# A hybrid decoder step: the first two columns of the recurrent input run over half the tokens first

## The chip, the cores and the metric

One core of one Trainium2 chip runs the whole program in one launch. The metric is the device time of that launch in microseconds (us), the median of the runs. The engines are named as in the profile: PE is TensorE, DVE is VectorE, ACT is ScalarE, POOL is GpSimd, and SP is the engine that issues nearly all transfers.

## The reference, cut to what matters

The model is one inference step of a two-layer decoder over 512 prompt tokens and 8 sample tokens, 520 in all, with 1024 channels. Layer 0 begins with an RG-LRU block:

```python
h = rms_norm(x, g_mix[0])
proj = h @ w_in                    # 1024 -> 2 * 1280
y = gelu(proj[..., :D_RNN])
xr = proj[..., D_RNN:]             # the recurrent input
xc = causal_dwconv(concat([conv_hist, xr]), conv_w, conv_b)   # width 4
r, i = sigmoid(xc blocks @ w_a + b_a), sigmoid(xc blocks @ w_x + b_x)
```

After it come the recurrence, its output product, a gated feed-forward block and an embedding, then a second layer with sparse attention. The change touches only the beginning: reading x, the first norm and the first three of the ten blocks of 128 channels of xr.

## The kernel before, in words

Activations stand with channels on the partitions: x is a tile of 128 partitions by 8 blocks by 520 tokens. Float32 products are made of three fast ones: each operand is split into a high part (ACT rounds it) and a low part (DVE subtracts the high part), and high times high, high times low and low times high are summed in PSUM. `split` (line 150) does this for weights, `xg_part` (line 500) for x times the norm's gain g_mix. The norm's other factor, one over the root mean square of a token, is multiplied in later, when a product leaves PSUM (`evac_scaled`, line 449).

One "column" is 128 output channels over all 520 tokens. `emit_k` (line 351) issues for each of the 8 blocks of input channels three products of two halves of 260 tokens: 48 matmuls a column, into one two-bank PSUM tile `MM`. There are three `MM` tiles and two one-bank tiles `TR`. `dense` (line 363) runs columns one after another. Its argument `at` hooks work in behind a block k of the first column. A column may start only when the `MM` tile of the column three before it has been read out.

The weights come through `Stream` (line 225). A chunk is loaded into one of three `RAW` tiles by SP, then split unit by unit (a unit is one column's weights) into `W` tiles, of which there are eight. The four row blocks of x (128 tokens by 1024 channels each) also stand in `W` tiles, and the 8 sample rows stand in a `RAW` tile whose other half is the scratch of the square sums.

Lines 510 to 550 are the fill. They stand in a block in which the order is written out by hand on each engine; instructions from outside the block may be put between by the planner. SP issues the identity matrix, x rows 0, the first 16 vectors, x rows 1, the sample rows, x rows 2, the first column's weights (`ws.load_to(0)`), x rows 3, the second column's weights (`add_second`), two tables and chunk 1. PE transposes a row block (`x_block`, line 187) by eight 128x128 transposes through the two `TR` tiles, and DVE or ACT copies each bank into x. Then `xg_part` splits blocks 0 to 3 of the first 256 tokens on ACT and DVE, blocks 4 to 7 on ACT and POOL, and all eight of the other 264 tokens on ACT and DVE. `x_square` (line 182) sums squares on ACT; four of the five stand behind all this, then `nm.root` makes the norm's factor on DVE. Three `dense` calls run columns 0, 1 and 2. Inside column 2, behind k = 1, `nm.bcast` (line 423) transposes the factor so that it stands beside the tokens, five PE transposes and two ACT copies.

Behind the block, `post_xr` (line 592) takes the three products out of PSUM, multiplied by that factor, and makes the convolution; columns 3 to 9 follow in the same way, then the gates. Small work that stands outside the block is `rg_scales` (line 205, some twenty DVE instructions on 128x10), the loading of the page table (line 572, eight small transfers on SP) and two DVE instructions on it (lines 575 and 576).

Of the kernel before, what the change touches and what calls it, by code (L numbers as in the profile page):

```python
# [20 lines left out]
NS = 8  # L21
# [93 lines left out]
def kernel(ctx: ExitStack, tc: tile.TileContext, I, O):  # L115
# [28 lines left out]
    def k3(ap, a):  # L144
        return ap.rearrange("p (a b) -> p a b", a=a)
# [40 lines left out]

    def x_block(tb):
        rows = 128 if tb < 4 else NS
        for q in range(0, 8, 4):
            ps = TR()  # L190
            for a in range(4):
                pe.transpose(ps[:, a * rows:(a + 1) * rows],
                             raws_x[tb][:rows, (q + a) * 128:(q + a + 1) * 128], ident[:rows, :rows])
            eng = act.copy if q and tb != 3 else dve.tensor_copy
            eng(x[:, q:q + 4, tb * 128:tb * 128 + rows], k3(ps[:, :4 * rows], 4))

    voff = {n: sum(r for _, r in VECS[:q]) for q, (n, _) in enumerate(VECS)}
    def V(name, i=0):
        c = voff[name] + i
        return vec[:, c:c + 1]  # L200
# [259 lines left out]

    # ---- weights, in the order in which the tensor engine takes them
    rgo = [("g", m) for m in range(10)] + [("y", m) for m in range(10)]
# [31 lines left out]

    # ---- layer 0, first norm, first columns of the recurrent input
    xg = [(T(F32R), T(F32R)) for _ in range(8)]
    xps, nm = [], Norm()
    ssq = sml[:, 48:53]

    def xg_part(j, c0, c1, eng):  # L500
        h, l = (t[:, c0:c1] for t in xg[j])
        act.activation(h, x[:, j, c0:c1], AF.Copy, scale=V("g_mix", j))
        if eng is dve:
            dve.scalar_tensor_tensor(l, x[:, j, c0:c1], V("g_mix", j), f32(h), op0=OP.mult, op1=OP.subtract)
        else:
            tm = T()[:, c0:c1]
            eng.tensor_mul(tm, x[:, j, c0:c1], V("g_mix", j).to_broadcast([128, c1 - c0]))
            eng.tensor_sub(l, tm, f32(h))

    with tc.manual_schedule():  # L510
        sp.dma_start(ident, I["consts"][:, 0:128])
        x_rows(0)
        sp.dma_start(vec[:, 0:16], I["vecs"][:, 0:16])
        x_rows(1)
        x_rows(4)
        x_rows(2)
        ws.load_to(0)
        x_rows(3)
        add_second()
        sp.dma_start(vec[:, 16:530], I["vecs"][:, 16:530])  # L520
        sp.dma_start(cst[:, 128:CCOS], I["consts"][:, 128:CCOS])
        ws.load_to(1)
        dve.memset(onesf, 1.0)
        dve.memset(ssq, 1.0)
        act.activation(sml[:, 40:41], onesf[:, 0:1], AF.Square)
        x_square(0, ssq)
        x_block(0)
        x_block(1)
        x_block(4)
        for j in range(4):  # L530
            xg_part(j, 0, 256, dve)
        x_block(2)
        ws.ahead(1)
        for j in range(4, 8):
            xg_part(j, 0, 256, pool)
        x_block(3)
        for j in range(8):
            xg_part(j, 256, NT, dve)
        ws.ahead(2)
        for tb in (1, 4, 2, 3):  # L540
            x_square(tb, ssq)
        y = nm.root(ssq)
        top, ws.stop = ws.stop, 2
        rst = []
        dense(1, 8, xg, lambda n, ps: xps.append(ps))
        dense(2, 8, xg, lambda n, ps: xps.append(ps), n0=1)
        ws.stop = 3
        dense(3, 8, xg, lambda n, ps: xps.append(ps), n0=2, at={1: lambda: rst.append(nm.bcast(y, 0))})
        rstd = rst[0]
        ws.stop = top  # L550

    # ---- states of the RG-LRU
    rg_t, rg_p, rg_o = T(), T(), T()
# [12 lines left out]

    # ---- page table, gathers
    pti = P.tile([128, 8], I32, name="pti")
# [15 lines left out]

    # ---- the recurrent input, its convolution
    st_c = k3(rg_o[:, 0:110], 11)
# [5 lines left out]
    def post_xr(m, ps):  # L592
        xr, xc = T(), T()
        pool.memset(xr[:, 0:3], 0.0)
        evac_scaled(xr[:, 3:3 + NT], ps, rstd)
        act.activation(xc[:, :NT], xr[:, 3:3 + NT], AF.Identity, scale=V("rg_conv_w", 30 + m), bias=V("rg_conv_b", m))
        pool.tensor_copy(st_c[:, :, m], xr[:, NP:NP + 11])
        xq.append((m, xr, xc))
        if m:
            conv_split(*conv_xr())  # L600
# [100 lines left out]

    # what the other engines do while the tensor engine is at each column of the gate branch
    SLOTS = ["e0 e1 r0 e2 r1 e3 r2", "e4 r3 e5 r4 e6 r5", "e7 r6 e8 r7 e9 r8 r9",
# [206 lines left out]

    # ---- compression weights
    w1h = [[T(F32R) for _ in range(4)] for _ in range(2)]
# [84 lines left out]

    # ---- token-major keys and values of the prompt and of the sample
    vst = [[T(F32R), T(F32R)] for _ in range(2)]
# [40 lines left out]

    # ---- compressed keys and values: the cache of the sample, then the prompt
    skh, skl = T(F32R), T(F32R)
# [309 lines left out]

    # ---- sample attention: scores
    kst, k0 = {}, {}
# [324 lines left out]

    # ---- first columns of the attention's output product, with the last heads  # L1680
    wo, wps = [], []
# [232 lines left out]
    yw, ys, fin = {}, [], {}  # L1914
    hcols = [(0, 256), (256, NT)]

# [136 lines left out]
```

## Time and profile before

| | |
|---|---|
| time, median of 3 runs | 1691.95 us (1690.61 to 1693.42) |
| the profiled execution: its time from first to last instruction (span) | 1690.5 us; the page gives no other time of it |
| lowest run less that span | 0.11 us |
| PE busy | 1628.7 us, 96% of the span |
| first matmul of a product starts | 15.50 us |
| last matmul of column 2 has started by | 35.70 us |

The span is read as the time between the program's first and last instruction; what a run has around it can be at most the difference to the lowest run, if both executions were alike. Times inside the program are us from the start of the span. A timeline row gives start, duration and count of like instructions that follow each other; what stands in brackets is how long the engine was idle before them and what ended that.

### The profile page before, as it was taken

The numbers are of one execution on the slowest core, as the hardware profiler recorded it, in microseconds if no ns is written. First come the engines' busy times: TensorE is split into PE (matmuls) and PEld (weight loads), VectorE is DVE, ScalarE is ACT, GpSimd is POOL, SyncE is SP. The second block draws the span as 40 slices with busy tenths as digits, with TensorE's granted clock in tenths as the row PEclk, the third lists the DMA queues.
The fourth block names the chain that finished last, engine by engine and source line by source line (L and its number), as shares of the span: only waits on it lengthen the run. The fifth ranks groups of instructions, "written<-read, shape, count | busy, mean of one in ns | idle before, by whom it ended". The sixth has DMA issues, their size and how long they took to land.

```text
span 1690.5 us, 32157 instructions
## 1 busy us (share of the span) xinstructions
PE 1628.7 (96%) x13089; PEld 1593.8 (94%) x13089; DVE 1081.3 (64%) x1794; ACT 795.7 (47%) x1455; POOL 410.9 (24%) x652
## 2 busy tenths in 40 slices
PE   7988999999999999999999999989999999999997
PEld 7988999999999999989999788869999999999997
DVE  6879647645654663665777878785576366466445
ACT  5674434423432444435743777783343144134434
POOL 2266411100100112321023466562111011001113
PEclk9999999999999999999998999999999999999998
DMA  6242343233233232334232213203332332332311
GB/s 197 86 148 89 107 128 93 83 101 93 82 101 95 81 113 81 96 120 142 80 123 100 94 41 116 76 26 85 101 90 85 100 91 85 101 90 85 112 32 51
DMA packets 197746, 160.81 MB, mean 95 GB/s; under 512 B 8160, under 2 KB 189872, under 8 KB 194760
## 3 DMA queue, kind: packets, MB, share of 16 engines
q1 hardware_dynamic: 194576, 136.74, 26.7%
q0 software_dynamic: 3024, 22.02, 3.6%
q8 instruction: 103, 1.69, 0.4%
q14 instruction: 43, 0.35, 0.1%
HBM read 154.41 MB, written 8.98 MB: 97 GB/s over the span
## 4 chain that ended last, share of the span: by engine, by line
PE 80%; DVE 8%; ACT 5%; issue 3%; POOL 2%; DMA 0%; SPq 0%; DVEq 0%; POOLq 0%; ACTq 0%
PE mm L355 62%; PE sc L355 2%; PE o L1648 2%; DVE w L155 1%; PE tr L1616 1%; ACT t L1590 1%; PE sc L1566 1%; ACT w L152 1%; PE tr L1516 1%; PE mm L1103 1%; PE mm L1104 1%; PE mm L1105 1%; DVE x L868 1%; PE tr L1087 1%; PE o L355 1%
## 5 line engine op out<-in xcount | busy, mean ns | idle before, releaser
L355 PE MATMUL mm<-t,w 128*128 128x260 f32 x9984 | 1214.9, 284 | 18.7 <-DVE t L455 9.8
L355 PEld LDWEIGHTS mm<-t,w 128*128 128x128 f32 x9984 | 1208.0, 189 | 21.5 <-issue 7.9
L152 ACT ACTIVATE w<-raw 128x1024 fp32r<-128x1024 f32 (+2 forms) x230 | 232.6, 1014 | 338.4 <-PE mm L355 287.0
L155 DVE TENSOR_TENSOR w<-raw,w 128x1024 fp32r<-128x1024 f32 (+2 forms) x230 | 282.5, 1232 | 65.3 <-ACT w L152 58.8
L455 DVE TENSOR_TENSOR t<-mm,t 128x520 f32<-128x520 f32 x138 | 95.6, 696 | 139.6 <-PE mm L355 136.0
L812 POOL COPY t<-t 128x10 f32<-128x10 f32 x96 | 24.0, 250 | 616.6 <-DVE t L455 616.6
L785 DVE TENSOR_TENSOR x<-x,mm 128x520 f32<-128x520 f32 x61 | 42.4, 696 | 170.2 <-PE mm L355 170.1
L815 DVE SCALAR_TENSOR_TENSOR t<-t,vec 128x512 f32<-128x512 f32 x192 | 143.1, 748 | 3.9 <-POOL t L812 0.7
L152 ACT ACTIVATE t<-t 128x520 fp32r<-128x520 f32 (+5 forms) x100 | 58.9, 593 | 182.8 <-DVE t L825 125.9
L155 DVE TENSOR_TENSOR t<-t 128x520 fp32r<-128x520 f32 (+5 forms) x100 | 69.1, 696 | 53.0 <-ACT t L152 52.7
L396 POOL TENSOR_TENSOR t<-t 128x520 f32<-128x520 f32 x35 | 57.5, 1644 | 171.2 <-ACT t L392 161.2
L155 DVE TENSOR_TENSOR w<-tr,w 128x512 fp32r<-128x512 f32 (+1 forms) x120 | 71.1, 612 | 27.1 <-ACT w L152 26.6
L813 ACT ACTIVATE t<-t,vec 128x520 f32<-128x520 f32 x96 | 78.8, 823 | 7.0 <-DVE t L455 7.0
L824 ACT ACTIVATE t<-t 128x520 f32<-128x520 f32 x48 | 30.6, 638 | 89.6 <-DVE t L815 89.5
L152 ACT ACTIVATE w<-tr 128x512 fp32r<-128x512 f32 (+1 forms) x120 | 60.6, 545 | 23.0 <-PE tr L1087 12.6
L1608 POOL TENSOR_TENSOR t<-t,sm 128x384 f32<-128x384 f32 (+1 forms) x64 | 59.8, 955 | 36.4 <-DVE sm L1600 18.5
L1590 ACT ACTIVATE t<-sc,sm 128x384 f32<-128x384 f32 (+3 forms) x120 | 63.1, 535 | 8.6 <-DVE sm L1577 4.6
L817 POOL TENSOR_TENSOR t<-t 128x8 f32<-128x8 f32 x96 | 46.7, 487 | 59.4 <-ACT t L813 59.2
L1616 PE MATMUL tr<-cst,t 128*128 128x128 f32 x320 | 56.2, 286 | 2.0 <-DVE sm L1600 2.0
L355 PE MATMUL sc<-t,w 128*128 128x260 f32 (+1 forms) x336 | 53.5, 283 | 0.7 <-ACT t L1108 0.7
L1566 PE MATMUL sc<-t 128*128 128x384 f32 (+1 forms) x128 | 41.1, 422 | 10.2 <-ACT t L1590 9.7
L152 ACT ACTIVATE t<-tr 128x128 fp32r<-128x128 f32 (+4 forms) x85 | 29.9, 374 | 40.9 <-PE tr L1316 18.8
(401 smaller groups left out, 1896.8 us busy)
## 6 DMA issues: line engine op xcount, KB each, us to landing
raw<-in_ffn_w_up SPq DMA_DIRECT2D x96, 512.0 KB
raw<-in_ffn_w_down SPq DMA_DIRECT2D x24, 1024.0 KB
raw<-in_ple_w_gate SPq DMA_DIRECT2D x8, 1024.0 KB
raw<-in_rg_w_in SPq DMA_DIRECT2D x12, 512.0 KB
raw<-in_rg_w_out SPq DMA_DIRECT2D x8, 640.0 KB
raw<-in_rg_w_in SPq DMA_DIRECT2D x4, 1024.0 KB
raw<-in_attn_w_qg SPq DMA_DIRECT2D x4, 1024.0 KB
t<-in_cache_win_kv SPq DMA_DIRECT2D x16, 256.0 KB
```

What stands on the lines that cost most here:

```text
L152: act.activation(hi, src, AF.Copy)
L155: (lo_eng or dve).tensor_sub(lo, src, f32(hi))
L355: pe.matmul(half(ps, hf)[:m, 0:HN], w[:, ki, :m], xx[:, hf * HN:(hf + 1) * HN], start=first and q == 0, stop=last and q == 2)
L396: (dve if self.n == 7 else pool).tensor_add(self.acc[:, :NT], self.acc[:, :NT], sq[:, :NT])
L455: dve.tensor_mul(halves(dst), ps[:m, :, 0:HN], halves(r[:m, :NT]))
L813: act.activation(t[:, :NT], up[:, 2:2 + NT], AF.Identity, scale=V("ffn_conv_w", 144 * i + 96 + j), bias=V("ffn_conv_b", 48 * i + j))
L815: dve.scalar_tensor_tensor(t[:, :NP], up[:, 2 - d:2 - d + NP], V("ffn_conv_w", 144 * i + (2 - d) * 48 + j), t[:, :NP], op0=OP.mult, op1=OP ...
L817: pool.tensor_add(t[:, NP:NT], t[:, NP:NT], pv[:, j, :])
L1566: pe.matmul(pss[br][:, 0:n], l, kst[br, g][q][:, 0:n], start=q == 0, stop=False)
L1590: act.activation(p[br][:, 0:n], sv[br], AF.Exp, bias=s[:, 0, br:br + 1], accum_out=s[:, 1, br:br + 1])
L1608: pool.tensor_mul(v, v, s[:, 3, br:br + 1].to_broadcast([128, n]))
L1616: pe.transpose(ps[:, j * 128:(j + 1) * 128], p[br][:, j * 128:(j + 1) * 128], ident)
```

## The change

The first two columns are computed first for the tokens 0 to 255, as soon as x rows 0 and 1 are there, and for the other 264 tokens afterwards.

- SP: the weights of the first two columns are issued behind x rows 1, ahead of the sample rows and x rows 2 and 3.
- x rows 0 and 1 are transposed into four PSUM banks (the two `TR` tiles and one `MM` tile), two channel blocks to a bank. ACT (`xg_hi`) and DVE (`xg_lo`) split x times gain straight from these banks. The copies into x come behind the splits, three on DVE and the last on ACT. POOL has no part in the fill any more.
- The weight splits of the first two columns are done in quarters of four blocks (`first_split`), the second column's into `T` tiles, and their order stands by hand between the other work. `first_mm` runs 24 matmuls of 256 (then 264) tokens into one bank of the column's `MM` tile.
- The sample rows and x rows 2 and 3 are transposed behind that, each before the next piece of products. The other 264 tokens are split when x rows 3 are copied.
- The square sums stand one behind each row block, and that of x rows 3 behind the weight split of column 2. `nm.bcast` moves from behind k = 1 to behind k = 5 of column 2.
- In `post_xr` the columns 0 and 1 are taken out of PSUM in two instructions, and without the raised priority of `evac_scaled`.

```diff
--- before.py
+++ after.py
@@ -184,15 +184,19 @@
         act.activation(raws_x[4][:rows, 1024:2048], raws_x[tb][:rows, 0:1024], AF.Square,
                        accum_out=out[:rows, tb:tb + 1])
 
-    def x_block(tb):
+    def x_t(ps, tb, j):
         rows = 128 if tb < 4 else NS
-        for q in range(0, 8, 4):
+        pe.transpose(ps, raws_x[tb][:rows, j * 128:(j + 1) * 128], ident[:rows, :rows])
+
+    def x_block(tb, engs):
+
+        rows = 128 if tb < 4 else NS
+        for q in range(0, 8, 4 if tb < 4 else 8):
+            n = 4 if tb < 4 else 8
             ps = TR()
-            for a in range(4):
-                pe.transpose(ps[:, a * rows:(a + 1) * rows],
-                             raws_x[tb][:rows, (q + a) * 128:(q + a + 1) * 128], ident[:rows, :rows])
-            eng = act.copy if q and tb != 3 else dve.tensor_copy
-            eng(x[:, q:q + 4, tb * 128:tb * 128 + rows], k3(ps[:, :4 * rows], 4))
+            for a in range(n):
+                x_t(ps[:, a * rows:(a + 1) * rows], tb, q + a)
+            engs[q // 4](x[:, q:q + n, tb * 128:tb * 128 + rows], k3(ps[:, :n * rows], n))
 
     voff = {n: sum(r for _, r in VECS[:q]) for q, (n, _) in enumerate(VECS)}
     def V(name, i=0):
@@ -492,64 +496,105 @@
     add_ffn(1)
     add_dense(I["ple_w_gate"][1], 8, 0, 8)
 
+
     xg = [(T(F32R), T(F32R)) for _ in range(8)]
     xps, nm = [], Norm()
     ssq = sml[:, 48:53]
 
-    def xg_part(j, c0, c1, eng):
-        h, l = (t[:, c0:c1] for t in xg[j])
-        act.activation(h, x[:, j, c0:c1], AF.Copy, scale=V("g_mix", j))
-        if eng is dve:
-            dve.scalar_tensor_tensor(l, x[:, j, c0:c1], V("g_mix", j), f32(h), op0=OP.mult, op1=OP.subtract)
-        else:
-            tm = T()[:, c0:c1]
-            eng.tensor_mul(tm, x[:, j, c0:c1], V("g_mix", j).to_broadcast([128, c1 - c0]))
-            eng.tensor_sub(l, tm, f32(h))
+    hcols = [(0, 256), (256, NT)]
+
+    def xg_hi(j, hf, src):
+        c0, c1 = hcols[hf]
+        act.activation(xg[j][0][:, c0:c1], src, AF.Copy, scale=V("g_mix", j))
+
+    def xg_lo(j, hf, src):
+        c0, c1 = hcols[hf]
+        dve.scalar_tensor_tensor(xg[j][1][:, c0:c1], src, V("g_mix", j), f32(xg[j][0][:, c0:c1]),
+                                 op0=OP.mult, op1=OP.subtract)
+
+    def first_mm(hl, ps, hf, k0, k1):
+        c0, c1 = hcols[hf]
+        for k in range(k0, k1):
+            h, l = (t[:, k % 4, :] for t in hl[k // 4])
+            for q, (w, xx) in enumerate(((h, 0), (h, 1), (l, 0))):
+                pe.matmul(ps[:, hf, 0:c1 - c0], w, xg[k][xx][:, c0:c1], start=k == 0 and q == 0,
+                          stop=k == 7 and q == 2)
 
     with tc.manual_schedule():
         sp.dma_start(ident, I["consts"][:, 0:128])
         x_rows(0)
         sp.dma_start(vec[:, 0:16], I["vecs"][:, 0:16])
         x_rows(1)
+        ws.load_to(0)
+        add_second()
         x_rows(4)
         x_rows(2)
-        ws.load_to(0)
         x_rows(3)
-        add_second()
         sp.dma_start(vec[:, 16:530], I["vecs"][:, 16:530])
         sp.dma_start(cst[:, 128:CCOS], I["consts"][:, 128:CCOS])
         ws.load_to(1)
         dve.memset(onesf, 1.0)
         dve.memset(ssq, 1.0)
         act.activation(sml[:, 40:41], onesf[:, 0:1], AF.Square)
+        raw = k3(ws.raws[0], 8)
+        t0, t1 = W(), W()
+        fw = [[tuple(k3(t, 8)[:, 4 * q:4 * q + 4, :] for t in (t0, t1)) for q in range(2)],
+              [tuple(k3(T(F32R)[:, 0:512], 4) for _ in range(2)) for q in range(2)]]
+
+        def first_split(n, q):
+            split(raw[:, 4 * q:4 * q + 4, n * 128:(n + 1) * 128], *fw[n][q])
+
+
+        banks = [TR(), TR()]
+        mm = MM()
+        banks += [mm[:, 0, :], mm[:, 1, :]]
         x_square(0, ssq)
-        x_block(0)
-        x_block(1)
-        x_block(4)
-        for j in range(4):
-            xg_part(j, 0, 256, dve)
-        x_block(2)
-        ws.ahead(1)
-        for j in range(4, 8):
-            xg_part(j, 0, 256, pool)
-        x_block(3)
+        for tb in range(2):
+            for j in range(8):
+                x_t(banks[j // 2][:, (j % 2) * 256 + tb * 128:(j % 2) * 256 + tb * 128 + 128], tb, j)
+        x_square(1, ssq)
+        xps.append(MM())
+        for r, bank in enumerate(banks):
+            src = k3(bank, 2)
+            for a in range(2):
+                xg_hi(2 * r + a, 0, src[:, a, :])
+            for a in range(2):
+                xg_lo(2 * r + a, 0, src[:, a, :])
+            if r < 2:
+                first_split(0, r)
+            if r < 3:
+                dve.tensor_copy(x[:, 2 * r:2 * r + 2, 0:256], src)
+            if r:
+                first_mm(fw[0], xps[0], 0, 2 * r - 2, 2 * r)
+        first_mm(fw[0], xps[0], 0, 6, 8)
+        act.copy(x[:, 6:8, 0:256], src)
+        del banks, bank, src, mm
+        x_block(4, (dve.tensor_copy,))
+        xps.append(MM())
+        for q in range(2):
+            first_split(1, q)
+        x_square(4, ssq)
+        x_block(2, (dve.tensor_copy, act.copy))
+        first_mm(fw[1], xps[1], 0, 0, 8)
+        x_square(2, ssq)
+        x_block(3, (dve.tensor_copy, act.copy))
         for j in range(8):
-            xg_part(j, 256, NT, dve)
-        ws.ahead(2)
-        for tb in (1, 4, 2, 3):
-            x_square(tb, ssq)
+            xg_hi(j, 1, x[:, j, 256:NT])
+            xg_lo(j, 1, x[:, j, 256:NT])
+        first_mm(fw[0], xps[0], 1, 0, 8)
+        first_mm(fw[1], xps[1], 1, 0, 8)
+        del raw, fw, t0, t1, ws.raws[0]
+        ws.nsplit = ws.used = 2
+        top, ws.stop = ws.stop, 3
+        ws.ahead()
+        x_square(3, ssq)
         y = nm.root(ssq)
-        top, ws.stop = ws.stop, 2
         rst = []
-        dense(1, 8, xg, lambda n, ps: xps.append(ps))
-        dense(2, 8, xg, lambda n, ps: xps.append(ps), n0=1)
-        ws.stop = 3
-        dense(3, 8, xg, lambda n, ps: xps.append(ps), n0=2, at={1: lambda: rst.append(nm.bcast(y, 0))})
+        dense(3, 8, xg, lambda n, ps: xps.append(ps), n0=2, at={5: lambda: rst.append(nm.bcast(y, 0))})
         rstd = rst[0]
         ws.stop = top
 
-    # ---- states of the RG-LRU
+
     rg_t, rg_p, rg_o = T(), T(), T()
     sp.dma_start(rg_t[:, 0:320], I["rg_state"])
     hst = rg_t[:, 0:240].rearrange("p (k m b) -> p k m b", k=3, m=10)
@@ -592,7 +637,11 @@
     def post_xr(m, ps):
         xr, xc = T(), T()
         pool.memset(xr[:, 0:3], 0.0)
-        evac_scaled(xr[:, 3:3 + NT], ps, rstd)
+        if m < 2:
+            for hf, (c0, c1) in enumerate(hcols):
+                dve.tensor_mul(xr[:, 3 + c0:3 + c1], ps[:, hf, 0:c1 - c0], rstd[:, c0:c1])
+        else:
+            evac_scaled(xr[:, 3:3 + NT], ps, rstd)
         act.activation(xc[:, :NT], xr[:, 3:3 + NT], AF.Identity, scale=V("rg_conv_w", 30 + m), bias=V("rg_conv_b", m))
         pool.tensor_copy(st_c[:, :, m], xr[:, NP:NP + 11])
         xq.append((m, xr, xc))
...
-    hcols = [(0, 256), (256, NT)]
```

## Rows read from the trace of the kernel before

**Rows 1.** The page: the span, the busy time of four engines (share of the span, instructions), and the shares of the chain of work that ended last.

```profile
span 1690.5 us, 32157 instructions
PE 1628.7 (96%) x13089; PEld 1593.8 (94%) x13089; DVE 1081.3 (64%) x1794; ACT 795.7 (47%) x1455; POOL 410.9 (24%) x652
...
PE 80%; DVE 8%; ACT 5%; issue 3%; POOL 2%; DMA 0%; SPq 0%; DVEq 0%; POOLq 0%; ACTq 0%
```

**Rows 2.** The timeline of PE from 4 to 45 us: start, us, instruction, count.

```profile
4.65 1.94 PE L192 MATMUL tr<-cst,w 128*128 128x128 f32 x8 [4.65 <-DMA w<-in_x_prompt]
7.14 1.57 PE L192 MATMUL tr<-cst,w 128*128 128x128 f32 x8 [0.55 <-DMA w<-in_x_prompt]
9.01 0.78 PE L192 MATMUL tr<-cst,raw 8*128 8x8 f32 x8 [0.30 <-DVE x L195]
9.72 1.09 PE L192 MATMUL tr<-cst,w 128*128 128x128 f32 x8
12.27 1.94 PE L192 MATMUL tr<-cst,w 128*128 128x128 f32 x8 [1.45 <-DMA w<-in_x_prompt]
15.50 13.69 PE L355 MATMUL mm<-t,w 128*128 128x260 f32 x100 [1.30 <-ACT t L502]
29.85 1.24 PE L355 MATMUL mm<-t,w 128*128 128x260 f32 x8 [0.66 <-DVE w L155]
30.93 0.60 PE L427 MATMUL tr<-cst,nrm 128*128 128x128 f32 x4
31.36 0.27 PE L430 MATMUL tr<-cst,nrm 128*128 128x128 f32 x1
```

**Rows 3.** The same view for the rest of column 2 alone (31.38 to 35.70 us): its last 36 matmuls.

```profile
31.39 4.58 PE L355 MATMUL mm<-t,w 128*128 128x260 f32 x36
```

**Rows 4.** Stretches of the fill: stretch, its us, busy us of PE, PEld, DVE, ACT and POOL (instructions), the granted share of PE's full clock (0.50 is 1.2 GHz, 1.00 is 2.4 GHz), the busy share of the DMA engines, GB/s.

```profile
4.60:6.60 2.00, 1.94 (x8) 1.57 (x8) 0.69 (x1) 1.15 (x2) 0.00 (x0) 1.00 0.90 304
8.20:11.60 3.40, 2.31 (x21) 1.76 (x19) 2.03 (x5) 2.35 (x7) 0.61 (x1) 1.00 1.08 354
11.60:15.00 3.40, 1.94 (x8) 1.57 (x8) 3.06 (x6) 3.10 (x8) 1.41 (x2) 0.50 1.10 352
15.00:18.40 3.40, 2.90 (x13) 2.87 (x14) 3.40 (x5) 3.40 (x9) 3.24 (x5) 0.50 0.59 195
18.50:28.40 9.90, 9.90 (x84) 9.90 (x83) 9.05 (x44) 7.89 (x13) 1.32 (x2) 1.00 0.49 163
```

**Rows 5.** The timeline of ACT, the rows of the operations that the change moves or repeats.

```profile
4.60 1.06 ACT L184 ACTIVATE raw<-w 128x1024 f32<-128x1024 f32 x1 [2.38 <-DMA w<-in_x_prompt]
5.57 0.19 ACT L184 ACTIVATION_READ_ACCUMULATOR raw<-w 128x1 f32 x1
...
9.91 1.71 ACT L502 ACTIVATE t<-x,vec 128x256 fp32r<-128x256 f32 x4
11.52 0.57 ACT L195 COPY x<-tr 128x512 f32<-128x512 f32 x1
11.98 1.06 ACT L152 ACTIVATE w<-raw 128x1024 fp32r<-128x1024 f32 x1
...
23.71 1.06 ACT L184 ACTIVATE raw<-w 128x1024 f32<-128x1024 f32 x1
...
31.56 0.59 ACT L428 COPY t<-tr 128x512 f32<-128x512 f32 x1 [1.81 <-PE tr L427]
32.05 0.17 ACT L431 COPY t<-tr 128x8 f32<-128x8 f32 x1
```

**Rows 6.** The timeline of DVE, the rows of the operations that the change moves or repeats.

```profile
9.46 0.19 DVE L195 COPY x<-tr 128x32 f32<-128x32 f32 x1 [0.50 <-PE tr L192]
10.46 1.68 DVE L504 SCALAR_TENSOR_TENSOR t<-x,vec,t 128x256 fp32r<-128x256 f32 x4 [0.80 <-ACT t L502]
...
13.08 1.23 DVE L155 TENSOR_TENSOR w<-raw,w 128x1024 fp32r<-128x1024 f32 x1 [0.34 <-ACT w L152]
14.22 1.28 DVE L195 COPY x<-tr 128x512 f32<-128x512 f32 x2
15.48 3.80 DVE L504 SCALAR_TENSOR_TENSOR t<-x,vec,t 128x264 fp32r<-128x264 f32 x5
...
19.84 1.29 DVE L504 SCALAR_TENSOR_TENSOR t<-x,vec,t 128x264 fp32r<-128x264 f32 x3
```

**Rows 7.** The timeline of DVE from the end of the norm's factor to the page table, and at the end of the ten columns.

```profile
28.49 0.16 DVE L419 SCALAR_TENSOR_TENSOR nrm<-nrm 128x5 f32<-128x5 f32 x1
28.57 4.63 DVE L155 TENSOR_TENSOR w<-raw,w 128x1024 fp32r<-128x1024 f32 x4
33.12 1.29 DVE L455 TENSOR_TENSOR t<-mm,t 128x520 f32<-128x520 f32 x2
...
40.29 0.17 DVE L575 CAST ptf<-pti 128x8 f32<-128x8 int32 x1 [3.31 <-DMA pti<-in_page_table]
...
42.50 0.69 DVE L455 TENSOR_TENSOR t<-mm,t 128x520 f32<-128x520 f32 x1
...
76.61 0.70 DVE L455 TENSOR_TENSOR t<-mm,t 128x520 f32<-128x520 f32 x1 [0.17 <-PE mm L355]
```

**Rows 8.** Two groups of `rg_scales` by line: count, then busy us and mean ns of one, then idle us before them.

```profile
L218 DVE TENSOR_SCALAR sml<-sml 128x10 f32<-128x10 f32 x7 | 1.2, 172 | 0.2
L217 DVE TENSOR_TENSOR sml<-sml 128x10 f32<-128x10 f32 x7 | 1.2, 170 | 0.2
```

**Rows 9.** The timeline of SP's queue: the loads of chunks 2 and 3 (one row), and the page table behind them.

```profile
22.58 2.67 SPq L282 DMA_DIRECT2D raw<-in_rg_w_in  x2
25.30 1.05 SPq L573 DMA_DIRECT2D pti<-in_page_table  x2
```

**Rows 10.** PE behind the ten columns: its timeline with the stalls of the gates, and the stretch 80 to 120 us with the columns of rows 4.

```profile
69.77 17.03 PE L355 MATMUL mm<-t,w 128*128 128x260 f32 x139
88.77 9.91 PE L355 MATMUL mm<-t,w 128*128 128x260 f32 x68 [1.97 <-ACT t L648]
100.53 6.02 PE L355 MATMUL mm<-t,w 128*128 128x260 f32 x48 [1.84 <-DVE t L610]
```

```profile
80.00:100.00 20.00, 16.71 (x124) 16.18 (x122) 14.23 (x11) 13.42 (x23) 17.20 (x12) 0.91 0.39 120
100.00:120.00 20.00, 17.11 (x140) 16.91 (x141) 14.60 (x12) 15.09 (x21) 12.89 (x9) 1.00 0.56 177
```

## The prediction

> **What bounds the kernel now.** I read the page first. PE is busy for 96% of the span and carries 80% of the chain that ended last [rows 1], so a microsecond counts only where it lets PE go on earlier. The change works in the first 36 us, so I read PE's timeline there next [rows 2]. Up to 15.50 us PE has only transposes, and it waits between them: for x rows, for the copies out of PSUM, and last for the split. From 15.50 us it is dense. 96 products of columns 0 and 1 and the first four of column 2 run to 29.19 us, 0.66 us are lost to a weight split on DVE, and column 2 ends with 36 matmuls from 31.39 us [rows 2, 3]. At 0.12 us each these are issued by 35.8 us, and column 3 follows without a gap. That is the mark to compare with: **before, column 3 starts at 35.8 us.** Behind it PE shows one run to 86.8 us [rows 10], and column 9 leaves PSUM at once when PE is done (DVE waited 0.17 us for it [rows 7]). So later or earlier by some microseconds at 35.8 us passes to the end one for one.
>
> The stretches show the clock [rows 4]: 13 matmuls took 2.90 us at 0.50 (0.22 us each), 84 took 9.90 us at 1.00 (0.12 us each). The half rate of the first 13 costs 1.3 us of the fill.
>
> **The change part by part.** *Start.* x rows 1 let PE go on at 7.14 us [rows 2], and the transfers ahead of them are the same. ACT now sums their squares at once, 1.16 us (4.60 to 5.76 us [rows 5]), so to 8.2 us. Two high parts at 0.43 us (four in 1.71 us) end at 9.1 us. No row shows ACT and DVE on one PSUM bank at the same time. If they may be, the low parts begin one high part earlier, at 8.7 us; I take 9.1 us, since the code sets both high parts of a bank ahead of its low parts. The Trainium skill, "PSUM — Partial Sum Buffer", section "Terms", says that two engines must not be on one bank at once, two readers included; by it 9.1 us holds and no gain is left here.
>
> *Weights.* They are 0.5 MB behind x rows 1. At the 304 to 354 GB/s of this stretch [rows 4] that takes 1.6 us and ends near 8.7 us, before ACT wants them at 9.1 us. The only sure upper bound is 11.98 us, when ACT split them before without waiting [rows 5]; I take 8.7.
>
> *DVE, the chain of the early half.* Eight low parts at 0.42 us (four in 1.68 us), two quarter splits at 0.62 us (half of 1.23 us), three copies at 0.64 us (two in 1.28 us) [rows 6]: 3.4 + 1.2 + 1.9 = 6.5 us, from 9.1 to 15.6 us. ACT needs 8 x 0.43 + 2 x 0.53 = 4.5 us beside it and stays ahead. A low part read from PSUM instead of SBUF has no row; copies from PSUM (0.64 us for 512) and subtractions from SBUF (0.62 us for 512) are alike, so I add nothing, with 8 x 0.1 us either way as bounds.
>
> *PE.* The first product can start at 9.1 + 0.84 + 0.62 = 10.6 us, 4.9 us earlier than before. But it is fed by DVE: six matmuls per pair of blocks, the last pair at 15.6 us. By 16.3 us (full clock) or 16.9 us (half) only 24 of 144 matmuls are done, 2.9 us of work at full clock. Then follow in PE's order:
> 1. sample rows, 0.78 us [rows 2], to 17.1 or 17.7 us. Only then DVE copies them (0.19 us) and subtracts the two quarters of column 1 (1.2 us), to 18.5 or 19.1 us.
> 2. x rows 2, eight transposes, 1.1 us at full and 1.9 us at half clock [rows 2], to 18.2 or 19.6 us. These cover the quarters.
> 3. 24 matmuls of column 1, 2.9 us, to 21.1 or 22.5 us.
> 4. x rows 3, 1.1 us, to 22.2 or 23.6 us.
> 5. A wait that is new: PE has nothing until the last bank is copied by ACT (0.57 us) and the first high part is made (0.43 us); with some 0.2 us for a transpose to end, 1.2 us. To 23.4 or 24.8 us. Before, this stood under the transposes of other blocks and a long lead of x.
> 6. 24 matmuls of column 0, the later half. PE needs 0.36 us a block, ACT gives one in 0.43 us; with the last low part 3.7 us, to 27.1 or 28.5 us.
> 7. 24 of column 1, 2.9 us, to 30.0 or 31.4 us. Under these lie the weight split of column 2 (1.06 us on ACT, 1.23 us on DVE), the last square and the norm's factor. Its DVE work ran under the old columns too and cost nothing; ended by 32 us, it is ahead of k = 5.
> 8. 48 of column 2 with the transposed factor, 5.8 + 0.5 us, to 36.3 or 37.7 us.
>
> POOL leaves the fill. Its gain shows on DVE: five low parts of 264 beside POOL took 3.80 us, three without it 1.29 us [rows 6], that is 0.33 us each. It isn't lost again, but before it lay under 0.22 us matmuls that were slower still, so it gives PE nothing.
>
> *Column 3.* It needs the PSUM tile of column 0. The factor is ready 0.85 us after its last transpose (31.36 to 32.22 us [rows 2, 5]), and DVE then needs about 0.7 us for two halves (two whole ones in 1.29 us [rows 7]); with k = 5 instead of k = 1 only 12 matmuls, 1.4 us, cover that. 0.2 us are left over; if DVE has just begun a weight split of 1.2 us, 1.4 us.
>
> *SP.* Chunk 3 goes into the tile of the sample rows and waits for the last square. That ends at 24.9 us before (23.71 us row, [rows 5]; SP's row [rows 9] lasts to 25.25 us) and near 29 us now. The page table is queued behind it, and DVE waits for that: 3.31 us to 40.29 us before [rows 7], to some 44 us now. Behind DVE's wait stands the reading of column 2, at 42.5 us before; column 5 needs it at 35.8 + 2 x 5.8 = 47.4 us, now 1.4 us later. 46.5 against 48.8 us: hidden, with 2.3 us in hand, and beyond that a microsecond for each.
>
> *Sum.* Column 3 starts at 36.5 us with the clock up early, at 37.9 us with it at half until 19.6 us: 0.7 or 2.1 us later than before. What starts 4.9 us earlier is used up by waits of the small early half. I take the middle, 1.4 us: 1690.5 + 1.4 = 1691.9 us against the profiled span of 1690.5 us. That span is 1.45 us under the median of the runs, 1691.95 us, so the median becomes **1693.3 us**; its own range is 1692.0 to 1695.0 us.
>
> **Rivals.** *The waits close.* If DVE and ACT keep up everywhere, PE needs from 16.3 us only 0.8 + 1.1 + 1.1 us of transposes, 120 x 0.12 = 14.4 us and 0.5 us: 34.2 us, 1.6 us earlier, so 1690.3 us. For it speaks that DVE is freed of POOL; against it that item 5 is a chain through three engines with nothing put beside it. More than that only comes if the gates behind fall better too: from 80 to 100 us the clock is 0.91 after a stall of 1.97 us, while 100 to 120 us has stalls of 1.84 us and more at 1.00 [rows 10]. A stall that keeps the clock gives back 0.09 x 20 = 1.8 us: 1688.5 us.
>
> *The clock stays down*, the rival on the other side. The row of 11.6 to 15.0 us has PE busy for 1.94 of 3.40 us and the clock at 0.50, and only a dense stretch, 2.90 of 3.40 us, ended with it up [rows 4]. The new early half is bursts of 1.3 us with pauses of 0.5 to 0.8 us. If column 1's 24 matmuls still run at 0.22 us, that is 24 x 0.1 = 2.4 us on the slower of my two paths: 2.1 + 2.4 = 4.5 us, 1696.4 us. It decides from about 18 us on: 24 matmuls in 5.2 us instead of 2.9 us. Against it: eight transposes alone took 1.94 us at 4.65 us and eight took 1.09 us at 9.72 us, so the clock had risen on transposes [rows 2]. The Trainium skill, "TensorE: Matmul & The Clock Gate", section "Part 4: PE-mode transpose", says that transposes don't count as activity for the clock; by it this rival would be the forecast. The trace differs, with the 1.94 and 1.09 us just named.
>
> *The small work lands on the chain.* The twenty instructions of `rg_scales` are placed by the planner; at 0.17 us and the idle between them [rows 8] about 0.2 us each. Between low parts they cost up to 4 us (1696 us); in DVE's pauses, around 16 and 20 us, nothing.
>
> *The change doesn't do what it says*: the weights come at 11.98 us, not 8.7. Then ACT stands 2.9 us before the second pair, and the whole fill slides: 1.4 + 2.9 us, 1696.2 us.
>
> **How the numbers follow.** Forecast 0.55, waits close 0.24 (half of it with the gates' gain), clock down 0.11, small work 0.05, weights late 0.05. About 0.2%, 3.4 us, is what a measurement of this kernel can tell from no change. Faster by more: only the gates' half, 0.12. Slower by more: clock, nearly all of the last two, and 0.03 of the forecast's upper end, 0.22. Within: 0.66. The range runs from 1689.3 us (waits closed, 1 us of scatter below 1690.3; the runs scatter by 1.4 us) to 1697.0 us (clock down).
>
> **What would show it.** First product near 10.6 us and 24 done by 16 to 17 us; DVE without a pause from 9.1 to 15.6 us; a PE pause of 1.2 us behind the transposes of x rows 3; column 3 at 36 to 38 us; DVE's page-table wait near 44 us and no PE stall from it. Wrong if column 3 starts before 35 us, if clock 0.50 reaches past 20 us, or if the time behind 40 us moves by more than the shift there.

## The result and the profile after

The changed kernel took 1701.11 us (median of 4 runs, 1699.52 to 1702.31) against 1691.28 us for the kernel before (4 runs beside it): a ratio of 1.0062, 95% interval 1.0050 to 1.0075. It is slower by some 10 us, where 1.4 us were forecast. The profiled run took 1702.31 us with a span of 1700.5 us: every run that lists both has 1.7 to 1.9 us around its span, so the 0.11 us worked out for this before was wrong, though the forecast doesn't hang on it. Its page, which answers to [rows 1]:

```profile
span 1700.5 us, 32148 instructions
PE 1634.6 (96%) x13089; PEld 1598.1 (94%) x13089; DVE 1082.4 (64%) x1802; ACT 795.8 (47%) x1456; POOL 405.6 (24%) x644
...
PE 80%; DVE 8%; ACT 5%; issue 3%; POOL 2%; DMA 1%; SPq 0%; DVEq 0%; POOLq 0%; ACTq 0%
```

The shares hardly moved: 10 us are 0.6% of the span. The place is seen only in PE's timeline, which answers to [rows 2, 3]:

```profile
8.76 1.12 PE L189 MATMUL tr<-cst,w 128*128 128x128 f32 x4 [1.54 <-DMA w<-in_x_prompt]
...
11.25 0.80 PE L520 MATMUL mm<-t,w 128*128 128x256 f32 x2 [0.52 <-ACT w L152]
...
17.60 1.43 PE L520 MATMUL mm<-t,w 128*128 128x256 f32 x5 [0.31 <-DVE t L512]
18.96 1.02 PE L189 MATMUL tr<-cst,raw 8*128 8x8 f32 x8
19.91 1.97 PE L189 MATMUL tr<-cst,w 128*128 128x128 f32 x8
21.53 4.92 PE L520 MATMUL mm<-t 128*128 128x256 f32 x24
...
28.41 3.88 PE L520 MATMUL mm<-t,w 128*128 128x264 f32 x24 [1.09 <-ACT t L508]
32.13 3.10 PE L520 MATMUL mm<-t 128*128 128x264 f32 x24
35.06 4.47 PE L359 MATMUL mm<-t,w 128*128 128x260 f32 x36
42.00 0.62 PE L431 MATMUL tr<-cst,nrm 128*128 128x128 f32 x4 [2.47 <-DVE nrm L423]
42.46 0.27 PE L434 MATMUL tr<-cst,nrm 128*128 128x128 f32 x1
42.49 53.59 PE L359 MATMUL mm<-t,w 128*128 128x260 f32 x432
```

Three things are to be seen. The early half ends at 18.96 us. The 24 matmuls of column 1 take 4.92 us, 0.21 us each, near the 0.22 us of the stretch at 0.50 in [rows 4] and not the 0.12 us of the one at 1.00, so PE still ran at its half clock (1.2 GHz). The view of stretches prints 1.00 here, but it does so too from 4.60 us before the change, where eight transposes took 1.94 us; in e1 below it prints 0.50 from 12.0 to 22.3 us, and there the transposes of x rows 2 take 1.97 us, as here. So the durations decide here. And ahead of the transposed factor PE waits 2.47 us for DVE. Behind that stall the clock falls once more:

```profile
42.70:46.10 3.40, 3.40 (x18) 3.40 (x17) 0.91 (x3) 1.85 (x4) 0.44 (x3) 0.50 0.69 253
```

The granted clock is 0.50 here. So the last 12 matmuls of column 2 go at 0.22 us, and column 3 starts at 45.1 us instead of 35.8. That is 9.3 us later. The ten columns end at 42.49 + 53.59 = 96.1 us against 86.8 us [rows 10], also 9.3 us later: up to there nothing of it is won back. Behind them the gates' 68 matmuls of [rows 10] take 8.43 us instead of 9.91, since the clock stays up there; it falls later (0.50 from 117.8 to 121.2 us), and the span is 10.0 us longer in the end.

Why the factor is late stands in DVE's timeline; before, its last step ended at 28.65 us, with the four weight splits behind it [rows 7]:

```profile
33.33 0.17 DVE L416 TENSOR_SCALAR nrm<-sml 128x5 f32<-128x5 f32 x1
...
33.61 0.16 DVE L418 TENSOR_SCALAR nrm<-nrm 128x5 f32<-128x5 f32 x1
36.71 0.17 DVE L620 CAST ptf<-pti 128x8 f32<-128x8 int32 x1 [2.94 <-DMA out_ffn_conv_sample<-in_state_ffn_conv]
...
37.33 1.22 DVE L155 TENSOR_TENSOR w<-raw,w 128x1024 fp32r<-128x1024 f32 x1
...
41.70 0.16 DVE L423 SCALAR_TENSOR_TENSOR nrm<-nrm 128x5 f32<-128x5 f32 x1
```

The planner now puts the page table's CAST between the third and the fourth of the factor's steps. It waits 2.94 us for transfers, and the rest of the factor waits behind it. (The releaser named is the transfer that landed last on that queue; CAST itself reads `pti`.) Then come three weight splits of 1.22 us among the remaining steps. ACT's timeline shows a second new wait, of 3.01 us, in front of the high parts of the fourth PSUM bank:

```profile
12.32 0.85 ACT L508 ACTIVATE t<-mm,vec 128x256 fp32r<-128x256 f32 x2
16.19 0.84 ACT L508 ACTIVATE t<-mm,vec 128x256 fp32r<-128x256 f32 x2 [3.01 <-DVE x L566]
```

It ends with DVE's copy out of the third bank. In the code, banks 3 and 4 are the two halves of one PSUM tile, `mm`. Last, SP's queue, which answers to [rows 9]:

```profile
22.04 0.39 SPq L286 DMA_DIRECT2D raw<-in_rg_w_in  x1
22.48 4.86 SPq L618 DMA_DIRECT2D pti<-in_page_table  x8
...
33.22 0.39 SPq L286 DMA_DIRECT2D raw<-in_rg_w_in  x1
```

and what SP waited for in the fill (total us, times, longest):

```profile
SPq L286 <- DVE t L155: 9.6, 1, 9.6
```

The page table stands ahead of the load at 33.22 us, but behind one that waited 9.6 us for DVE's split of column 1.

### The profile page after: what moved, and what is told of

Same layout as the page of the kernel before. It is cut to its first block, busy times and chain, and to the rows that moved or that the text cites. A ratio compares the mean times of both kernels' runs of the same rounds, so it can differ in the third digit from the quotient of the medians.

```text
span 1700.5 us, 32148 instructions
## 1 busy us (share of the span) xinstructions
PE 1634.6 (96%) x13089; PEld 1598.1 (94%) x13089; DVE 1082.4 (64%) x1802; ACT 795.8 (47%) x1456; POOL 405.6 (24%) x644
## 4 chain that ended last, share of the span: by engine, by line
PE 80%; DVE 8%; ACT 5%; issue 3%; POOL 2%; DMA 1%; SPq 0%; DVEq 0%; POOLq 0%; ACTq 0%
PE mm L359 62%; PE sc L359 2%; PE o L1697 2%; PE tr L1665 1%; DVE w L155 1%; PE sc L1615 1%; ACT t L1639 1%; PE tr L1565 1%; PE mm L1152 1%; ACT w L152 1%; PE mm L1153 1%; PE mm L1154 1%; DVE x L917 1%; PE tr L1136 1%; PE o L359 1%
## 5 line engine op out<-in xcount | busy, mean ns | idle before, releaser
L359 PE MATMUL mm<-t,w 128*128 128x260 f32 x9888 | 1202.1, 284 | 18.0 <-DVE t L459 10.9
L359 PEld LDWEIGHTS mm<-t,w 128*128 128x128 f32 x9888 | 1195.4, 189 | 20.3 <-issue 9.7
```

The costliest lines, as they stand in the source:

```text
L359: pe.matmul(half(ps, hf)[:m, 0:HN], w[:, ki, :m], xx[:, hf * HN:(hf + 1) * HN], start=first and q == 0, stop=last and q == 2)
```

## The experiments

All are compared with runs of the kernel before on the same chip. A profile is one run of several, and runs of one kernel differ by 5 us either way, so times are read from the ratios and places from the traces.

**e1: the page table's two DVE instructions behind the gates.**

```
-    dve.tensor_copy(ptf, pti)
-    dve.tensor_scalar(idx, ptf, 16.0, ...)
...
         slot(10)
+        dve.tensor_copy(ptf, pti)
+        dve.tensor_scalar(idx, ptf, 16.0, ...)
```

> The changed kernel with the two DVE instructions on the page table taken from behind the fill to the end of the gates' block. Theory A (the page table's conversion, queued on DVE in the middle of the norm's factor, holds the factor): the factor is ready some 3 us earlier (38.9 instead of 41.9 us), PE does not stall behind k = 5 of column 2 (2.47 us gone) and its clock does not fall there (about 1.6 us gone): 4 us off, 1697.0 us. Theory B (the three weight splits of 1.2 us that stand between the steps of the factor hold it, and the conversion only fills time): stall and time stay, 1700.8 us.

1694.31 us, ratio 1.0015 (1.0004 to 1.0026). Theory A's mechanism holds, not its size: 4 us were expected, and by the ratios nearly 8 came back. The splits stay among the steps, yet the factor is ready at 36.3 us and PE doesn't wait for it, nor does the clock fall:

```profile
32.82 4.47 PE L359 MATMUL mm<-t,w 128*128 128x260 f32 x36
37.13 0.60 PE L431 MATMUL tr<-cst,nrm 128*128 128x128 f32 x4
```

By the ratios three quarters of the loss hang on where one CAST of 0.17 us stands. In the two traces column 3 starts 5.9 us earlier, at 39.2 us: 2.47 us are the stall, 1.0 us the clock behind it, 0.9 us the matmuls of column 1 (4.04 us here), and 1.4 us only that x rows 1 came earlier (PE goes on at 7.40 instead of 8.76 us).

**e2: the fourth bank in a PSUM tile of its own.**

```
         mm = MM()
-        banks += [mm[:, 0, :], mm[:, 1, :]]
+        mm2 = MM()
+        banks += [mm[:, 0, :], mm2[:, 0, :]]
```

> The changed kernel with the fourth transposed bank in a PSUM tile of its own. Theory A (ACT's wait of 3.01 us before the last two high parts comes from the third and fourth bank being one tile): the wait is gone, the last low parts end 1.0 us earlier (16.9 instead of 17.9 us), the early half too, and column 2 starts up to 1 us earlier. The time itself then moves by 0 to 1 us (1700.1 to 1701.1 us), since the factor still waits for the page table. Theory B (ACT would have waited for something else): nothing moves.

1693.06 us, ratio 1.0017 (1.0003 to 1.0032): far more than expected. ACT's wait is gone, and the clock is up by column 1:

```profile
11.21 1.57 ACT L508 ACTIVATE t<-mm,vec 128x256 fp32r<-128x256 f32 x4
```

```profile
17.47 3.08 PE L520 MATMUL mm<-t 128*128 128x256 f32 x24
...
29.41 4.47 PE L359 MATMUL mm<-t,w 128*128 128x260 f32 x36
36.13 0.62 PE L431 MATMUL tr<-cst,nrm 128*128 128x128 f32 x4 [2.24 <-DVE nrm L423]
```

CAST still waits 3.11 us, but it ends at 32.97 us, not 36.71, and SP's load ahead of the page table goes out at 18.25 us, not 22.04:

```profile
18.25 0.39 SPq L286 DMA_DIRECT2D raw<-in_rg_w_in  x1
...
32.97 0.17 DVE L621 CAST ptf<-pti 128x8 f32<-128x8 int32 x1 [3.11 <-DMA out_ffn_conv_sample<-in_state_ffn_conv]
```

So either repair alone gives back 7 to 8 of 10 us. That asked for an explanation, and two were tried below: the clock, or one chain of waits with both in it.

**e3: the order of the first transfers as before**, in the changed kernel.

```
-        ws.load_to(0); add_second(); x_rows(4); x_rows(2); x_rows(3)
+        x_rows(4); x_rows(2); ws.load_to(0); x_rows(3); add_second()
```

> The changed kernel with the transfers in the order of the kernel before. Theory A (issuing the weights right behind x rows 1 makes x rows 1 land 1.6 us later, but the weights are what the first product needs): x rows 1 let PE go on at 7.1 us again, the weights land near 10.8 us and hold ACT there, so the early half ends within 0.5 us of where it does now; 1700.6 to 1701.6 us. Theory B (x rows 1 decide): everything 1.6 us earlier, 1699.5 us.

1702.73 us, ratio 1.0065 (1.0044 to 1.0085), as after the whole change. The first product waits 2.23 us for ACT's split of the later weights, starts at 11.48 us, and the stall at the factor grows to 4.29 us. The order of the transfers isn't the cause.

**e4: the new order of the first transfers alone**, in the kernel before (the edit of e3 the other way round).

> The kernel before with the transfers in the order of the changed one, nothing else. Theory A (it delays x rows 1 from 7.1 to 8.7 us and x rows 2 and 3, on which the fill before depends): the first product starts at 16.5 to 17 us instead of 15.5 us, 1692.3 to 1693.0 us against 1691.3 us. Theory B (the fill hides it): 1691.3 us.

1695.65 us, ratio 1.0030 (1.0013 to 1.0046), more than either theory. The sample rows land at 10.92 us and the first product comes at 17.93 us instead of 15.50. And the page table shows up again, now ahead of the reading of column 0:

```profile
38.92 0.17 DVE L575 CAST ptf<-pti 128x8 f32<-128x8 int32 x1 [3.42 <-DMA t<-in_rg_state]
39.12 0.23 DVE L576 TENSOR_SCALAR idx<-ptf,cst 128x8 int32<-128x8 f32 x1
39.26 1.30 DVE L455 TENSOR_TENSOR t<-mm,t 128x520 f32<-128x520 f32 x2
```

Column 3 stalls for 1.86 us on that reading.

**e5: e1 and e2 together.**

> The changed kernel with both repairs: the page table's two DVE instructions behind the gates' first slots (as in e1) and the fourth bank of transposes in a PSUM tile of its own (as in e2). Theory A (two separate causes, one at the front of the fill, one at the norm's factor): column 2 starts at 29.4 us as in e2; the factor, 35.98 us in e2 behind a wait of 3.11 us for the page table, is ready near 32.9 us, just when PE comes to k = 5, so that the stall of 2.24 us goes and column 3 starts at 35.7 to 36.1 us. Time 2.2 us under e2: 1690.5 to 1691.5 us, no different from the kernel before. Rival B (the two repairs remove the same wait, and whichever stands alone has all of the gain): 1693 to 1694 us, with a stall of 1 us or more left ahead of the transposed factor.

1691.81 us, ratio 1.0005 (0.9992 to 1.0018): level with the kernel before, as theory A said. The absolute time missed its range by 0.3 us. The profiled run was the slowest of 11 (1695.85 us, column 2 at 32.7 us), so its places are late; it has no stall at the factor.

**e6: e5 with the factor's steps kept together by hand.**

```
-        ws.ahead()
         x_square(3, ssq)
+        ws.ahead()
         y = nm.root(ssq)
+        ws.stop = 6
+        ws.ahead()
```

> e5, with the last square ahead of the split of column 2's weights, and the splits of the next three weight blocks written out by hand behind the root steps, so that nothing stands between these on DVE. Theory A (with the page table gone the three splits of 1.2 us between the root steps are hidden under the five blocks of column 2): the factor is ready near 30 us instead of 33 us, nothing starts earlier, 1690.5 to 1691.5 us, within 0.5 us of e5. Rival B (the factor is still what PE waits for in e5): 0.5 to 2 us faster than e5. Rival C (the splits pushed back are late for columns 3 and 4): a stall on DVE's split at 36 us or 42 us and up to 2 us slower.

1696.46 us, ratio 1.0037 (1.0024 to 1.0050). The factor is ready at 31.6 us, which nobody needed. But the planner now sets a fourth split, whose buffers come free only with column 2, ahead of the reading of column 0:

```profile
37.79 1.23 DVE L155 TENSOR_TENSOR w<-raw,w 128x1024 fp32r<-128x1024 f32 x1 [2.78 <-ACT w L152]
38.94 1.43 DVE L643 TENSOR_TENSOR t<-mm,t 128x256 f32<-128x256 f32 x4
```

```profile
39.84 8.35 PE L359 MATMUL mm<-t,w 128*128 128x260 f32 x55 [2.93 <-DVE t L643]
```

Rival C's mechanism at another place: a waiting instruction queued ahead of one that PE needs, with 2.93 us for it. Rival C had up to 2 us; some 5 us were measured against e5. In the traces the gates' 68 matmuls take 9.95 us here and 8.43 us in e5, the clock once more.

**e7: e1 with 16 transposes of the identity in PE's pauses.**

```
+                pe.transpose(xps[1][:, 1, 0:128], ident, ident)
```

> e1 (page table late), with the fourth bank still in the shared tile, but with 4 transposes of the identity into an unused PSUM bank ahead of each later group of the early half and behind the last one, 16 in all: work that nobody reads, put where PE waits. Theory A (what the early half's pauses cost is above all the clock: it stays at half until 22.3 us in e1): the clock rises by 18 us, the 24 matmuls of column 1 take 3.1 us instead of 4.04 us, the transposes of x rows 2 take 1.1 instead of 1.97 us, column 2 starts 1.0 to 2.0 us earlier than e1's 32.8 us, and the time is 1692.3 to 1693.3 us. Rival B (the pauses themselves are the loss, the clock follows from elsewhere): column 2 at 32.8 us or later by what the 16 transposes take beyond the pauses, up to 1 us, and 1694.3 to 1695.3 us.

1693.58 us, ratio 1.0020 (1.0008 to 1.0032). In the trace, of the fastest of 12 runs, theory A holds: the 24 matmuls of column 1 take 3.08 us, column 2 starts at 31.4 us. In the times no gain over e1 can be told, so this one didn't decide.

**e8: the kernel before with the page table's two instructions moved as in e1.**

> The kernel before with the page table's two DVE instructions moved behind the gates' first slots, as e1 does it in the changed kernel. Theory A (before, DVE's wait of 3.31 us for the page table lay in time that DVE had to spare): no change, 1690.3 to 1692 us. Rival B (that wait cost the kernel before as well, through the columns that DVE reads behind it): 1 to 3 us faster, and the stall of PE in front of some column before 50 us is gone.

1693.38 us, ratio 1.0017 (1.0005 to 1.0029). Neither theory: not faster, so nothing shows that the wait before cost anything, but slower by some 3 us (0.8 to 4.9 us by the interval), and the trace names no new stall. In the profiled run the x rows came 1.0 us later than in [rows 2] and PE was slow until 22.6 us, which is scatter of one run. Why the median rose stays open. It bears on e1, e5, e7 and e10, which carry the same move: like with like, on the same chip, e5 took 1691.81 us against 1693.38 us here, and the intervals of their ratios overlap.

**e9: the 16 transposes alone**, in the changed kernel: the clock mended, the waits not.

> The changed kernel with nothing but the 16 transposes of the identity that fill PE's pauses in the early half (as in e7): the page table's instructions stay ahead of the norm's factor on DVE, and the fourth bank stays in the shared tile. It tells apart why e2 alone gave back 8 us. Theory A (a chain of waits: DVE's quarter splits of column 1 end near 22.0 us because of the shared tile, SP's next weight transfer waits for them, the eight page-table transfers are queued behind it, DVE's page-table wait ends 14.7 us after that issue, and the factor behind it; the clock changes nothing in this chain): the clock comes up before 20 us, column 2 starts 1 to 3 us earlier than 35.1 us, but the factor is still ready at 41 to 43 us, the stall of PE at k = 5 grows by what column 2 gained, column 3 starts at 43 to 45 us and the time stays at 1699 to 1702.5 us. Rival B (the clock that stayed at half was what e2 mended): the time falls as in e2, to 1693 to 1696 us, and column 3 starts before 40 us.

1699.89 us, ratio 1.0041 (1.0028 to 1.0054): in theory A's range, above theory B's, though by the ratio some 3.5 us under the changed kernel, with intervals that overlap, so the clock may have a part of its own. The trace, of the slowest of 6 runs, shows the chain of waits:

```profile
19.08 1.09 PE L189 MATMUL tr<-cst,w 128*128 128x128 f32 x8
19.93 3.06 PE L520 MATMUL mm<-t 128*128 128x256 f32 x24
...
31.70 4.47 PE L359 MATMUL mm<-t,w 128*128 128x260 f32 x36
41.24 1.09 PE L431 MATMUL tr<-cst,nrm 128*128 128x128 f32 x4 [5.07 <-DVE nrm L423]
```

Column 2 starts 3.4 us earlier than after the change, and the stall grows from 2.47 to 5.07 us: column 3 starts at 44.9 us, where it did. The chain can be followed from run to run. SP's load, held by DVE's split of column 1, issues at 22.04 us after the change, 18.25 us in e2, 22.01 us in e3 and 20.71 us here; CAST's wait ends at 36.71, 32.97, 37.10 and 35.71 us, always 14.7 to 15.1 us later. What moves the head of the chain is not the shared tile alone. PE goes on at x rows 1 at 7.40 us in e1, 7.29 us in e2 and 7.00 us in e5, and SP's load issues at 20.67, 18.25 and 19.32 us; the clock is down to 22.3 us in e1 and to 22.6 us in e5, but up by column 1 in e2. Of the 3.8 us between the changed kernel and e2, 1.5 us are thus the scatter of x rows 1, about 1 us the tile (e1 against e5) and the rest goes with the clock (e5 against e2). This is an estimate from one trace of each.

**e10: e5 with the 16 transposes.**

> e5 (both repairs) with the same 16 transposes of the identity in the early half's pauses. Theory A (after both repairs nothing but PE's own work and the clock is left in the fill): the clock comes up by 15 us in every run instead of between 14.7 and 22.6 us, column 2 starts at 29.4 to 30.5 us, column 3 at 35.7 to 36.9 us, and the time is 1 to 2 us under e5, 1689.8 to 1690.8 us, level with the kernel before. Rival B (the transposes take from the fill what the clock gives): the same as e5, 1691.3 to 1692.3 us. Neither expects a time that beats the kernel before by a measurable amount.

1692.44 us against 1692.25 us before, ratio 1.0004 (0.9993 to 1.0014): level with the kernel before again, and no different from e5. Column 2 starts at 30.2 us, column 3 at 36.6 us. Nothing tried here beats the kernel before.

## Why the prediction was wrong

*The sum fits a fill without two waits that were missed, not the one that ran.* Column 2 started at 35.06 us, where the working has 30.0 or 31.4 us, and took 10.0 us to column 3, where it has 6.3 us. So about half of the 7.2 us beyond the slower path's 37.9 us lies in the fill (ACT's wait, the half clock, the late x rows 1), and half in the stall at the factor and the clock behind it. With both waits gone (e5, e10) the change costs 0.4 to 0.5 in a thousand, 0.7 to 0.8 us, not distinct from nothing, where 1.4 us were worked out. e10's column 3, 36.6 us, lies at the lower of the two forecast values, 36.5 us. What the change costs or gives by itself stays open within some 3 us, since both runs carry the move that e8 found slower in the kernel before.

1. *"Ended by 32 us, it is ahead of k = 5" is the step that failed.* The factor was ready at 41.9 us, with the page table's wait of 2.94 us and three weight splits of 1.22 us among its steps. I took its place in DVE's order from the trace of before, where only three instructions of `rg_scales`, of 0.16 or 0.17 us, stood among them. That order is the planner's, and the change moved it. With the page table gone and the splits still there (e1), the factor is in time.
2. *"The page table is queued behind it [chunk 3]", DVE's wait near 44 us, hidden: wrong in place and in price.* The table was issued at 22.48 us, ahead of chunk 3, and its wait stood in front of the factor instead of a column's reading. e1 prices it: 6.8 us between the medians, nearly 8 us by the ratios, of which its trace places only a part.
3. *"ACT needs 4.5 us beside it and stays ahead" failed.* It waited 3.01 us. I asked only whether two engines may share one bank; here two banks of one tile were taken in turn, and e2 shows that it goes with a tile of its own. The early half ends at 18.96 us against 16.03 us in e2, but 1.5 us of that is x rows 1. The rest of its price is the chain: later splits of column 1, later page table, later factor. With the chain cut, e5 against e1, it is worth 0.1%, with intervals that overlap.
4. *The clock.* The rival "the clock stays down" came true in the profiled run: 24 matmuls in 4.92 us, 1.8 us more than the 3.08 us of e2, against 2.4 us forecast. But e9 shows that it doesn't carry most of the loss: mended alone, the ratio goes from 1.0062 to 1.0041 with intervals that overlap, while e1 and e2 reach 1.0015 and 1.0017.
5. *Start and weights.* x rows 1 let PE go on at 8.76 us instead of 7.14, in other runs of this order at 7.00 us (e5) to 8.39 us (e9): scatter. The first product came at 11.25 us (10.6 forecast).
6. *Right:* the new wait behind x rows 3, 1.09 us (1.2); the later half of column 0, 28.41 to 32.13 us, 3.7 us (3.7); column 1, 2.9 us (2.9); `rg_scales` in DVE's pauses, though three of them (20.16 to 20.64 us) stand ahead of the splits of column 1, at the head of the chain; and a shift of column 3 that reaches the end, 9.3 us there and 10.0 us in the span. One pair of traces can't show that one for one: in the twelve profiled runs the time from column 3 to the end lies between 1650 and 1659 us.

Why two repairs of 7 to 8 us don't add up to 15: both cut the same chain, once at its head (the split of column 1) and once at its tail (CAST ahead of the factor).

## What to carry to other kernels

In a queue that works in order, an instruction of 0.17 us costs what it waits for to everything behind it: ask of each small wait which queue it stands in, what stands behind it, and whether a planner will set it at the same place after the change. Check what two engines share by tile as well as by bank. And when two repairs each give back nearly all, look for one chain with both in it before adding them up.

## What the runs showed of the hardware

The page table is eight transfers of 0.5 KB. While they were under way, the DMA engines moved almost nothing: these are the packets and the rate of the changed kernel from 20 to 40 us, the rate in slices of 0.5 us, and slices 14 to 28 (26.5 to 34 us) are nearly empty.

```profile
GB/s 0 0 0 0 0 0 78 281 383 385 391 385 194 3 0 1 0 0 33 0 1 0 0 0 0 1 0 0 50 49 156 238 201 291 360 379 385 387 255 176
DMA packets 3438, 2.53 MB, mean 127 GB/s; under 512 B 1206, under 2 KB 3428, under 8 KB 3428
```

The 4 KB are 1024 numbers of 4 bytes, and some 1200 packets were under 512 B, so they went about one number to a packet. They took some ten microseconds (26.5 to 36.71 us, where CAST's wait ends), at the end of a chain that PE waited for. The Trainium skill, "DMA: Bandwidth & Descriptors", section "Rules for kernel authors", asks to coalesce many small transfers, since under 64 KB one pays mostly overhead; this trace agrees, with 0 to 3 GB/s in most of those slices against 381 to 391 in a weight load.

The clock came up with the transposes of the identity and without them. With the 16 transposes of the identity (e7, e9, e10) the eight transposes of x rows 2 took 1.09 us each time; without them 1.97 us after the change, in e1, e3 and e5, but 1.09 us in e2 and e6. So it was up by then in three of three runs against two of six, and the transposes may hold or raise it. The Trainium skill, "TensorE: Matmul & The Clock Gate", section "Part 4: PE-mode transpose", has it that transposes don't count as activity in the same way. The kernel before differs from it: only transposes stood between eight that took 1.94 us and eight that took 1.09 us [rows 2]. In e7, e9 and e10 matmuls stood between them, so these three decide nothing here.

Runs of one kernel scatter with the mean clock that they are granted: the 25 of the kernel before beside e1 to e4 went from 1685.23 us at 0.990 to 1695.54 us at 0.984, and most of the faster ones have the higher clock.
